# Bonus sums of a head pair as four float32 products on 32-column strips instead of two products with ones

## The chip, the cores and the metric

The kernel runs on one core of a Trainium2 chip. The metric is the device time of one execution in microseconds; three runs of the kernel before give a median of 993.13 us (991.97 to 993.62). Engines are called PE (matrix products), PEld (its weight loads), DVE (vector), ACT (scalar, activations), POOL (general) and SP (which issues most of the DMA transfers). Each engine has its own list of instructions and runs it in order; engines wait for one another by semaphores.

## What is computed

One layer of a hybrid encoder for 512 tokens behind 16 meta tokens, width 2048. One input projection gives the columns of two branches: a recurrence of 16 heads of 64 (RWKV-7) and a gated convolution. The part that matters here:

```python
kk = kk / maximum(norm(kk, axis=-1), 1e-12)        # per head and token: the key norm
k  = k * (1.0 + (a - 1.0) * k_a)
y  = recurrence(r, decay, k, v, kk, kk * a)
bonus = sum(r * k * r_k, axis=-1) * v              # per head and token: a sum over the head's 64 channels
y_a = (groupnorm(y) + bonus) * silu(g_r)
y_b = B * conv3(C * h) * silu(g_c)
h_res = h_res + concat(y_a, y_b) @ w_out
```

Both the key norm and the bonus are sums over the 64 channels of a head. Channels lie on partitions (two heads, a head pair, fill the 128), so such a sum goes over partitions and is done by PE as a product with a matrix of zeros and ones.

## The kernel before

**Projections.** 65 tiles of 128 output columns are streamed through PE, each as products over 16 slices of 128 inputs. A weight quarter (128 x 512) is split into a rounded high half and the rest as low half, and every product is made of three: high by high, high by low, low by high (`steps`, `pieces`). Raw weights come by SP into three buffers `wr` of two quarters (L159); ACT casts a quarter's high half (L151), DVE subtracts for the low half (L152), into six buffers `hl`. Names like w50 count these quarters; quarter 4j+q belongs to tile j of the plan. The plan runs k, r, v of two head pairs, their g, and then a convolution group C, h, B, gc; the first such group has B ahead of the plan.

**PE's order is written by hand.** `fill(ns)` takes projection products from the stream until their planned time is used up; between the calls stand the products of the head pairs. The time table `FW` sets how much projection work lies between them. The order of DVE, ACT, POOL and SP is made by a scheduler from priorities: `ahead()` raises a block of instructions, and weight splits are raised too.

**Head pairs.** `prepare(i)` does pair i, `invert` two of them. In `prepare`, after the low-rank paths, DVE forms the operands `ar` and `bk` and the product `r = r * hv * ta` (L734, the elementwise bonus). PE then makes the gram products (L754) and, in `gram_meta`, the key norms: four float32 products of 144 columns (L786), each with 32 columns of the constants as weights and each on its own strip of 32 columns of PE (`tile_position`), into one bank at columns 96 to 239. ACT copies them to `n2` (L779). SP sends `n2` to DRAM (`sn`), and reads it back spread over 72 partitions as `nd`; so the gram blocks go through `sg` and come back as `d`.

**The bonus before.** `split` casts r to its rounded half (ACT, L664) and subtracts (DVE, L665). After the gram products, two products of 512 columns with the 128 x 128 matrix `ones` (L818, L819; 1 within a head, 0 elsewhere) write the sums into the bank `zb`, already spread over the channels; ACT copies the bank to r (L820). DVE multiplies r by v (L917), and SP stores it for later (L918).

**Inversion.** From `nd` and `d`, DVE inverts 16 x 16 blocks, 72 at a time: two rows on nd (L853, L854), a copy to y (L859), tt and y (L860, L861), then for m = 2, 4, 8 blocks of four dependent rows: product, sum, product, sum (L871 to L886). The last row of a pair is the sum of 512 numbers per partition. y goes to DRAM (`sx`, L901) and comes back as `xT` and `xo` (L892, L893); DVE turns xT into `xn` (L946), and PE uses xn in the products t (L961), first for the even pair, then for the odd one. These steps have planned times on a clock that counts PE's products: the store of y at 29000 ns for an even pair and 20500 (22500 for pair 1) for an odd one.

**Convolution.** DVE takes C from its two banks to u (a row ex for four edge columns, and two rows u), later h to hh in the same way (L402, L403); POOL multiplies u by hh (L484); ACT makes cv (L486) and DVE adds two taps (L489). At the end of a group of two pairs the chain of the odd pair and this convolution share DVE with the splits.

Of the kernel before, what the change touches and what calls it, by code (L numbers as in the profile page):

```python
# [9 lines left out]
F32 = mybir.dt.float32  # L10
F32R = mybir.dt.float32r
I32 = mybir.dt.int32
AF = mybir.ActivationFunctionType
ALU = mybir.AluOpType
# [4 lines left out]
P = 128  # L19
DM = 2048  # L20
KT = DM // P
SEQ = 512
META = 16
L = SEQ + META
CH = 64
# [7 lines left out]
C_ID, C_GM, C_BM, C_ON = 0, 128, 384, 512  # L33
# [11 lines left out]
    tr=3200, lev=3000, cp=4200, out=1500, begin=19500, p=2900, u=2900, s=4200, mid=1000, last=3700, mix=2600,  # L45
# [44 lines left out]
def hymba_kernel(ctx: ExitStack, tc: tile.TileContext, xt, xtok, front, w_in, w_out, pv, lup, cst, msk, gf, out):  # L90
    nc = tc.nc
    ctx.enter_context(tc.manual_schedule(engines={mybir.EngineType.PE}))
    cp = ctx.enter_context(tc.tile_pool(name="cp", bufs=1))
    dp = ctx.enter_context(tc.tile_pool(name="dp", bufs=2, space=DRAM))
# [3 lines left out]
    cs = cp.tile([P, C_N], F32, name="cs")  # L98
# [13 lines left out]
    def col(off, i=0):  # L112
        return pvt[:, off + i : off + i + 1]
# [55 lines left out]
    xp = ph1.enter_context(tc.tile_pool(name="xp", bufs=1))  # L169
# [3 lines left out]
    rst = xp.tile([P, 4], F32, name="rst")  # L173
    rsx = cq.tile([P, 2 * META], F32, name="rsx")
    la = cq.tile([P, 2, L], F32R, name="la")
    ones = xp.tile([P, P], F32R, name="ones")
    omm = xp.tile([P, 33], F32, name="omm")
    hv = xp.tile([P, 6, 8], F32, name="hv")
    hl = cp.tile([P, 2, 8], F32, name="hl")
# [3 lines left out]
    pi = ph1.enter_context(tc.tile_pool(name="pi", bufs=1, space=PSUM))  # L183
# [5 lines left out]
    def tr(name, dt=F32):  # L189
        return cq.tile([P, LP], dt, tag="tr", name=name, bufs=5)  # L190
# [121 lines left out]
    with tc.issue_after(head):  # L312
        nc.vector.tensor_scalar(
            out=omm, in0=pvt[:, V_MU : V_MU + 33], scalar1=-1.0, scalar2=1.0, op0=ALU.mult, op1=ALU.add
        )
        for d, off in (
# [4 lines left out]
                out=d, in0=pvt[:, off : off + 8], scalar1=0.5, scalar2=None, op0=ALU.mult  # L321
            )
        nc.vector.tensor_scalar(
            out=hv[:, 4], in0=pvt[:, V_KA : V_KA + 8], scalar1=-0.5, scalar2=1.0, op0=ALU.mult, op1=ALU.add
        )

    nc.scalar.copy(ones, cs[:, C_BM : C_BM + P])
    FULL = ((0, 272), (272, L))
    TAIL = ((14, 272), (272, L))
    REAL = ((META, L),)  # L330
# [44 lines left out]
    def next_banks():  # L375
        what, i = plan[state["tile"] + 1]
        return [pm.tile([P, 512], F32, tag="main", name=f"ps_{what}{i}_{r}") for r in range(2)]
# [236 lines left out]
    def fill(ns):  # L614
        while ns > 0:
            seen = len(ready)
            t = step()
            if t is None:
                return
            ns -= t  # L620
            if len(ready) > seen:
                ns += FW["evac"]
# [23 lines left out]
    def ahead():  # L646
        return tc.high_priority(offset=AHEAD)

    def c3(t):
        return t.rearrange("p (c s) -> p c s", s=CH)  # L650
# [7 lines left out]
        nc.vector.tensor_tensor(out=lo, in0=raw, in1=hi.bitcast(F32), op=ALU.subtract)  # L658
        return hi, lo

    def split(t, name, n):
        hi = tr(f"{name}_h", F32R)[:, 0:n]
        lo = tr(f"{name}_l", F32R)[:, 0:n]
        nc.scalar.copy(hi, t)  # L664
        nc.vector.tensor_tensor(out=lo, in0=t, in1=hi.bitcast(F32), op=ALU.subtract)  # L665
        return hi, lo

    heads = [(h, slice(64 * h, 64 * h + 64), slice(64 - 64 * h, 128 - 64 * h)) for h in range(2)]

    place = [(i % 2) * 4 + i // 2 for i in range(NPAIR)]  # L670
# [11 lines left out]
    def behind(dst, src):  # L682
        with tc.issue_after(state["dma"]):
            nc.sync.dma_start(dst, src)
# [5 lines left out]
    def second_level(z):  # L690
        return [t[:, 256:512].rearrange("p (q k s) -> p q k s", q=2, s=32) for t in z]

    def prepare(i):
# [22 lines left out]
            out=bk[:, :, 0], in0=c3(k), scalar=hv[:, 2, i : i + 1], in1=c3(te), op0=ALU.mult, op1=ALU.mult  # L716
# [3 lines left out]
            out=ta, in0=ta, scalar1=hv[:, 3, i : i + 1], scalar2=hv[:, 4, i : i + 1], op0=ALU.mult, op1=ALU.add  # L720
        )
        nc.vector.scalar_tensor_tensor(
            out=ar[:, :, 0], in0=c3(k), scalar=col(V_KK, i), in1=e1[:, :, 0:CH], op0=ALU.mult, op1=ALU.mult
# [6 lines left out]
        r = got["r", i]  # L730
        nc.vector.tensor_tensor(
            out=ar[:, 1:NCH, 1], in0=c3(r), in1=e1[:, 1:NCH, 1 : CH + 1], op=ALU.mult
        )
        nc.vector.scalar_tensor_tensor(  # L734
            out=r, in0=r, scalar=hv[:, 5, i : i + 1], in1=ta[:, CH:LP], op0=ALU.mult, op1=ALU.mult
        )

        sq = tr(f"sq{i}")
        nc.scalar.activation(sq, k, AF.Square, scale=col(V_KK, i))
        rh, rl = split(r, f"rk{i}", SEQ)  # L740
        fill(FW["gram_b" if p else "gram"] + FW["meta"].get(i, 0))

        late = state["step"] > 48
# [16 lines left out]

        def gram_meta():
            z = early or next_banks()
            norms = key_norms(z[0][:, 96 : 96 + NS])
            for h, hs, ho in heads:
                nc.tensor.matmul(
                    z[h][:, 0:META],
                    bk[hs, 0, h : h + 2, :].rearrange("p a s -> p (a s)"),
                    ar[hs, 0, 0, 0:META],
                    start=True, stop=True,
                )  # L770
            if p and "levels" in state:
                state["out"] = state.pop("levels").pop(0)(second_level(z))
            with ahead():
                for h in range(2):
                    nc.vector.tensor_tensor(
                        out=gt[:, h, 0, 0:META], in0=z[h][:, 0:META], in1=gmask[:, h, 0:META], op=ALU.mult
                    )
            with ahead():
                nc.scalar.copy(n2, norms)  # L779
            if "out" in state:  # L780
                state.pop("out")()
            state["banks"] = z

        def key_norms(z):
            for j in range(4):
                nc.tensor.matmul(  # L786
                    z[32 * j : 32 * j + 32], cs[:, C_BM + 48 : C_BM + 80], sq[:, j * NS : (j + 1) * NS],
                    start=True, stop=True, tile_position=(0, 32 * j),
                )
            return z  # L790
# [11 lines left out]

        NS = LP // 4
        n2 = tr(f"n2{i}")[:, 0:NS]
        if late:
            gram_meta()
        za = [pz.tile([P, 4, P], F32, tag="tz", name=f"g{i}_1_{h}") for h in range(2)]
# [3 lines left out]
        if not late:  # L811
            gram_meta()
# [1 line left out]
        masked(zc, 5, 9)  # L814
        fill(FW["gram2"] - FW["meta"].get(i, 0))

        zb = pi.tile([P, SEQ], F32, tag="ser", name=f"zb{i}")
        nc.tensor.matmul(zb, ones[:, 0:P], rh, start=True, stop=False)  # L818
        nc.tensor.matmul(zb, ones[:, 0:P], rl, start=False, stop=True)  # L819
        nc.scalar.copy(r, zb)  # L820
        fill(FW["misc"])


# [4 lines left out]
        sg = dp.tile([SCR], F32, tag="sg", name=f"sg{i}")  # L828
        sn = dp.tile([2 * LP], F32, tag="sn", name=f"sn{i}")
        sx = scr_x[i % 2]  # L830

        def rows(t, h):
            return bass.AP(tensor=t.tensor, offset=t.offset + h * NCH * 4 * BLK, ap=[[CH, CH], [4 * BLK, NCH], [1, CH]])

        def blocks(t):
            return bass.AP(tensor=t.tensor, offset=t.offset, ap=[[BLK, 8 * NCH], [CH, 16], [1, 16]])

        for h in range(2):
            behind(sn[h * LP : (h + 1) * LP].rearrange("(j s) -> j s", s=NS), n2[16 - 16 * h : P : 32])
        for h in range(2):  # L840
            behind(rows(sg, h), gt[64 * h : 64 * h + 64, h, :, 0:CH])
        NB = 8 * NCH
# [5 lines left out]
        nd = cq.tile([NB, 16], F32, tag="nd", name=f"nd{i}")  # L848
        behind(d, blocks(sg))
        behind(nd, sn.rearrange("(p s) -> p s", s=16))  # L850
        y = cq.tile([NB, 256], F32, tag="y", name=f"y{i}").rearrange("p (s t) -> p s t", t=16)
        nc.gpsimd.memset(y, 0.0)
        nc.vector.tensor_scalar(out=nd, in0=nd, scalar1=1e-24, scalar2=None, op0=ALU.max)  # L853
# [9 lines left out]
        def sub(x, r0, c0, dims):  # L863
            return bass.AP(tensor=x.tensor, offset=x.offset + r0 * 16 + c0, ap=[list(x.ap[0])] + dims)

        for m in (2, 4, 8):
            for b in range(16 // (2 * m)):
# [4 lines left out]
                    out=pq,  # L872
                    in0=sub(d, o, o + m, [[16, m], [0, m], [1, m]]),
                    in1=sub(y, o + m, o + m, [[0, m], [1, m], [16, m]]),
                    op=ALU.mult,
                )
                nc.vector.tensor_reduce(
                    out=tq.rearrange("p (i j) -> p i j", i=m), in_=pq, op=ALU.add, axis=AX.X
                )
                nc.vector.tensor_tensor(  # L880
                    out=pq,
                    in0=sub(y, o, o, [[16, m], [0, m], [1, m]]),
                    in1=bass.AP(tensor=tq.tensor, offset=tq.offset, ap=[list(tq.ap[0]), [0, m], [1, m], [m, m]]),
                    op=ALU.mult,
# [19 lines left out]
        for h, hs, ho in heads:  # L904
            for b in range(2):
                for a in range(2):
                    later(9000 + 900 * (4 * h + 2 * b + a), lambda h=h, b=b, a=a: nc.sync.dma_start(
                        bass.AP(
                            tensor=bd.tensor,
                            offset=bd.offset + (h ^ a) * (NCH - 1) * CH * NPAIR * P + place[i] * P + 64 * h + 32 * b,  # L910
                            ap=[[NPAIR * P, 32], [32 * NPAIR * P, 2 * NCH - 2], [1, 32]],
# [11 lines left out]
        for b in range(4):  # L923
            for t in range(2):
                later(14000 + 1000 * (2 * b + t), lambda b=b, t=t: nc.sync.dma_start(
                    bass.AP(
                        tensor=vd.tensor,
                        offset=vd.offset + (64 * (1 - b // 2) + 32 * t) * NPAIR * CH + place[i] * CH + 32 * (b % 2),
                        ap=[[NPAIR * CH, 32], [P * NPAIR * CH, NCH], [1, 32]],
# [264 lines left out]
    for i in range(0, NPAIR, 2):  # L1194
        invert([prepare(i), prepare(i + 1)])
# [161 lines left out]
    def here(t, n):  # L1357
        return xa[t][:, n * 512 : (n + 1) * 512] if n < 2 else xb[n - 2][:, t]
# [153 lines left out]
    z = {}  # L1512
# [55 lines left out]
    with tc.manual_schedule(engines={mybir.EngineType.DVE, mybir.EngineType.Activation, mybir.EngineType.Pool}):  # L1568
# [16 lines left out]
        for part in range(2):  # L1585
            cols = slice(256 * part, 256 * part + 256)
            for jj in range(8):
                hi, lo = right[(1, "M2", jj // 2), jj % 2]
# [4 lines left out]
            h = here(1, 2)[:, cols]  # L1593
# [70 lines left out]
```

## Time and profile before

| | before |
|---|---|
| median of three runs | 993.13 us (991.97 to 993.62) |
| span of the profiled execution | 991.2 us |
| PE busy | 981.2 us (99%) |
| DVE busy | 707.8 us (71%) |
| ACT busy | 390.4 us (39%) |
| two products with ones, each | 0.39 us, x8 |
| ACT: cast for the split / copy of the sums | 0.62 / 0.587 us, x8 each |
| DVE: subtraction for the split / product with v | 0.69 / 0.69 us, x8 each |

The span is that of one execution under the profiler; times of runs are a little longer, since they hold what lies around the span. A row in order of time gives the start, the duration, the engine, the line, what is written from what, the shape, and in brackets how long the engine had been idle ahead of it and for whom it had waited. Durations of matmuls overlap: what a matmul costs PE is the distance from its start to the start of the next one. Buffer numbers are left out in the profile (w for w50, y for y1).

### The profile page before, as it was taken

What the parts mean: (1) busy time and instruction counts of PE and PEld (TensorE: products, weight loads), DVE (VectorE), ACT (ScalarE), POOL (GpSimd) and SP (SyncE); (2) the same over time, 40 slices, a digit from 0 to 9 for tenths busy, and PEclk for the clock granted to TensorE, in tenths of its full rate; (3) what the DMA queues carried; (4) which work ended last, traced back from release to release, by engine and by line L of the source; (5) the groups of instructions that cost most, each with busy time, mean ns of one, the idle gap of its engine ahead of it and who ended that gap; (6) DMA issues with size and microseconds to landing.
All of it is one profiled execution on the core that took longest, in us unless ns stands there. A gap on an engine that the chain in (4) does not pass through costs nothing.

```text
span 991.2 us, 23393 instructions
## 1 busy us (share of the span) xinstructions
PE 981.2 (99%) x9511; PEld 907.4 (92%) x9511; DVE 707.8 (71%) x1413; ACT 390.4 (39%) x731; POOL 128.0 (13%) x242
## 2 busy tenths in 40 slices
PE   9999999999999999999999999999999999999996
PEld 8999999999998999998999998889889898788885
DVE  6777966578675679653779654465756697998897
ACT  7553432344322434322434323232332435546464
POOL 0110302012010121010111010011211102001001
PEclk9999999999999999999999999999999999999999
DMA  9526576246675385853375856988886697697654
GB/s 324 156 91 149 145 202 160 88 126 150 152 181 166 92 194 117 211 150 107 87 186 122 205 143 189 280 250 250 229 252 189 179 281 197 183 313 197 149 128 170
DMA packets 205387, 176.89 MB, mean 178 GB/s; under 512 B 138528, under 2 KB 168032, under 8 KB 204768
## 3 DMA queue, kind: packets, MB, share of 16 engines
q1 hardware_dynamic: 202688, 166.50, 60.2%
q0 software_dynamic: 2304, 8.39, 4.9%
q8 instruction: 74, 1.21, 0.5%
q10 hardware_dynamic: 288, 0.52, 0.1%
q14 instruction: 33, 0.27, 0.1%
HBM read 139.02 MB, written 36.35 MB: 177 GB/s over the span
## 4 chain that ended last, share of the span: by engine, by line
PE 94%; DVE 3%; DMA 1%; ACT 1%; issue 1%; SPq 0%; DVEq 0%; POOL 0%; ACTq 0%
PE ps_v L352 9%; PE ps_h L352 9%; PE ps_C L352 9%; PE ps_g L352 9%; PE ps_gc L367 9%; PE ps_B L367 9%; PE ps_k L352 8%; PE ps_r L352 8%; PE M L1381 5%; PE P L1381 4%; PE Q L1381 2%; PE g L754 2%; PE ps_lora L367 1%; PE ps_k L367 1%; PE zy L1139 1%; PE ps_r L367 1%
## 5 line engine op out<-in xcount | busy, mean ns | idle before, releaser
L151 ACT CAST w<-wr 128x512 fp32r<-128x512 f32 x252 | 153.7, 619 | 285.8 <-PE ps_C L352 47.5
L152 DVE TENSOR_TENSOR w<-wr,w 128x512 fp32r<-128x512 f32 x252 | 175.3, 707 | 117.7 <-ACT w L151 116.7
L352 PE MATMUL ps_v<-xh,w 128*128 128x256 f32 (+2 forms) x512 | 84.0, 285 | 0.0
L367 PE MATMUL ps_B<-xh,w 128*128 128x512 f32 x256 | 83.4, 394 | 0.0
L352 PE MATMUL ps_h<-xh,w 128*128 128x256 f32 (+2 forms) x512 | 81.6, 281 | 0.0
L352 PE MATMUL ps_g<-xh,w 128*128 128x256 f32 (+2 forms) x512 | 81.5, 281 | 0.0
L367 PE MATMUL ps_gc<-xh,w 128*128 128x512 f32 x256 | 81.1, 392 | 0.0
L352 PE MATMUL ps_C<-xh,w 128*128 128x256 f32 (+2 forms) x512 | 80.8, 280 | 0.0
L352 PEld LDWEIGHTS ps_v<-xh,w 128*128 128x128 f32 x512 | 73.9, 188 | 0.3
L352 PE MATMUL ps_k<-xh,w 128*128 128x256 f32 (+1 forms) x448 | 73.4, 285 | 0.0
L352 PE MATMUL ps_r<-xh,w 128*128 128x256 f32 (+1 forms) x448 | 72.6, 281 | 0.0
L352 PEld LDWEIGHTS ps_h<-xh,w 128*128 128x128 f32 x512 | 72.1, 189 | 0.3
L352 PEld LDWEIGHTS ps_g<-xh,w 128*128 128x128 f32 x512 | 72.0, 189 | 0.4
L352 PEld LDWEIGHTS ps_C<-xh,w 128*128 128x128 f32 x512 | 71.7, 189 | 0.2
L352 PEld LDWEIGHTS ps_k<-xh,w 128*128 128x128 f32 x448 | 64.7, 188 | 0.4
L352 PEld LDWEIGHTS ps_r<-xh,w 128*128 128x128 f32 x448 | 63.5, 189 | 0.2
L352 PE MATMUL ps_h<-xl,w 128*128 128x256 f32 x256 | 57.3, 281 | 0.0
L367 PEld LDWEIGHTS ps_gc<-xh,w 128*128 128x128 f32 x256 | 47.8, 188 | 10.0
L367 PEld LDWEIGHTS ps_B<-xh,w 128*128 128x128 f32 x256 | 47.8, 188 | 9.7
L352 PE MATMUL ps_C<-xl,w 128*128 128x256 f32 x256 | 56.2, 280 | 0.0
L352 PE MATMUL ps_v<-xl,w 128*128 128x256 f32 x256 | 55.8, 278 | 0.0
L352 PE MATMUL ps_g<-xl,w 128*128 128x256 f32 x256 | 55.5, 278 | 0.0
(382 smaller groups left out, 2143.6 us busy)
## 6 DMA issues: line engine op xcount, KB each, us to landing
wr<-in_w_in_dram SPq DMA_DIRECT2D x126, 512.0 KB
ct<-opd SPq DMA_DIRECT2D x72, 192.0 KB
wo<-in_w_out_dram SPq DMA_DIRECT2D x24, 512.0 KB
x<-in_w_out_dram POOLq DMA_DIRECT2D x16, 512.0 KB, 5.7
opd<-ar SPq DMA_DIRECT2D x8, 576.0 KB
opd<-gt SPq DMA_DIRECT2D x16, 288.0 KB
bd<-bt SPq DMA_DIRECT2D x64, 64.0 KB
bw<-bd SPq DMA_DIRECT2D x16, 256.0 KB
```

Source lines behind the costliest of these rows:

```text
L151: nc.scalar.copy(hi, rq)
L152: low[q] = eng.tensor_tensor(out=lo, in0=rq, in1=hi.bitcast(F32), op=ALU.subtract).ins
L352: nc.tensor.matmul(ps[r][:, 0 : b - a], ww[:, k * P : (k + 1) * P], xx[:, kt, a:b], start=(kt == 0 and n == 0), stop=(kt == KT - 1 and n = ...
L367: nc.tensor.matmul(ps[r], ww[:, w], xx[:, kt, a:b], start=(kt == 0 and n == 0), stop=(kt == KT - 1 and n == 2))
L754: nc.tensor.matmul(z[h][:, c - c0], bk[hs, c, h : h + 2, :].rearrange("p a s -> p (a s)"), ar[hs, c].rearrange("p a s -> p (a s)"), start= ...
L1139: nc.tensor.matmul(zy[e][hs if e else ho, k], t[hs, o : o + CH], x, start=(n == 0), stop=(n == 2))
L1381: nc.tensor.matmul(bank[s], left(prod, jj, m, s), w, start=(jj == 0 and n == 0), stop=(jj == 7 and n == 2))
```

## The change

The matrix `ones`, `split`, the bank `zb`, the two products and the copy back from the bank are taken out. The sums of the bonus are now made like the key norms, right behind them: four float32 products of 128 columns on four strips, straight from r, into the pair's second bank. The function for both is `head_sums`. ACT copies the 128 columns to `nb`; SP stores four rows of it per head in `sb` and reads `sb` back into r, each head's row of 512 numbers spread over its 64 partitions (source pattern 2 x 64 times the same x 512). The product r times v waits for that transfer.

```diff
-    ones = xp.tile([P, P], F32R, name="ones")
...
-    nc.scalar.copy(ones, cs[:, C_BM : C_BM + P])
...
-    def split(t, name, n):
-        hi = tr(f"{name}_h", F32R)[:, 0:n]
-        lo = tr(f"{name}_l", F32R)[:, 0:n]
-        nc.scalar.copy(hi, t)
-        nc.vector.tensor_tensor(out=lo, in0=t, in1=hi.bitcast(F32), op=ALU.subtract)
-        return hi, lo
...
-        rh, rl = split(r, f"rk{i}", SEQ)
...
-            norms = key_norms(z[0][:, 96 : 96 + NS])
+            norms = head_sums(z[0][:, 96 : 96 + NS], sq, NS)
+            bonus = head_sums(z[1][:, 96 : 96 + P], r, P)
...
                 nc.scalar.copy(n2, norms)
+                nc.scalar.copy(nb, bonus)
...
-        def key_norms(z):
+        def head_sums(z, x, n):
             for j in range(4):
                 nc.tensor.matmul(
-                    z[32 * j : 32 * j + 32], cs[:, C_BM + 48 : C_BM + 80], sq[:, j * NS : (j + 1) * NS],
+                    z[32 * j : 32 * j + 32], cs[:, C_BM + 48 : C_BM + 80], x[:, j * n : (j + 1) * n],
                     start=True, stop=True, tile_position=(0, 32 * j),
                 )
...
-        zb = pi.tile([P, SEQ], F32, tag="ser", name=f"zb{i}")
-        nc.tensor.matmul(zb, ones[:, 0:P], rh, start=True, stop=False)
-        nc.tensor.matmul(zb, ones[:, 0:P], rl, start=False, stop=True)
-        nc.scalar.copy(r, zb)
...
+        sb = dp.tile([2 * SEQ], F32, tag="sb", name=f"sb{i}")
...
+        for h in range(2):
+            behind(sb[h * SEQ : (h + 1) * SEQ].rearrange("(j s) -> j s", s=P), nb[16 * h : P : 32])
...
         behind(nd, sn.rearrange("(p s) -> p s", s=16))
+        behind(r, bass.AP(tensor=sb.tensor, offset=sb.offset, ap=[[SEQ, 2], [0, CH], [1, SEQ]]))
```

PE's list changes only by these products; `FW` is as before. The scheduler's lists are others. In the rows below, the names carry buffer numbers, and the engine that a row waits for stands in brackets. The lines after the change are 6 or 7 lower than before.

DVE in the first convolution group, where the inversion of pair 1 meets h0 and gc0. Before, the last rows of y1 lie around hh0, the evacuation of h0:

```order
L871 TENSOR_TENSOR prod1_1872<-d1_1864,y1_1868 72x512 [waits DVE_49]
L877 TENSOR_REDUCE tt1_1873<-prod1_1872 72x64 [waits DVE_49]
L880 TENSOR_TENSOR prod1_1872<-y1_1868,tt1_1873 72x512 [waits DVE_49]
L403 TENSOR_TENSOR hh0_2136<-ps_h0_0_2016,rs_116 128x256 [waits PE_49]
L886 TENSOR_REDUCE y1_1868<-prod1_1872 72x8x8 [waits DVE_49]
L402 TENSOR_TENSOR ex_2137<-ps_h0_1_2017,rst_117 128x4 [waits PE_49,Pool_49]
L403 TENSOR_TENSOR hh0_2136<-ps_h0_1_2017,rs_116 128x256
L152 TENSOR_TENSOR w50_2010<-wr25_2008,w50_2010 128x512 [waits DMAHW2_49,Activation_49]
```

After, hh0 stands much earlier in y1's chain (behind three of its four smallest blocks), and the splits of w50 and w51 stand behind the chain's last row:

```order
L879 TENSOR_REDUCE y1_1870<-prod1_1874 72x2x2 [waits DVE_49]
L401 TENSOR_TENSOR hh0_2138<-ps_h0_0_2018,rs_116 128x256 [waits PE_49]
L864 TENSOR_TENSOR prod1_1874<-d1_1865,y1_1870 72x8 [waits DVE_49]
L870 TENSOR_REDUCE tt1_1875<-prod1_1874 72x4 [waits DVE_49]
L873 TENSOR_TENSOR prod1_1874<-y1_1870,tt1_1875 72x8 [waits DVE_49]
L879 TENSOR_REDUCE y1_1870<-prod1_1874 72x2x2 [waits DVE_49]
L864 TENSOR_TENSOR prod1_1874<-d1_1865,y1_1870 72x64 [waits DVE_49]
L870 TENSOR_REDUCE tt1_1875<-prod1_1874 72x16 [waits DVE_49]
L400 TENSOR_TENSOR ex_2139<-ps_h0_1_2019,rst_117 128x4 [waits PE_49,Pool_49]
L401 TENSOR_TENSOR hh0_2138<-ps_h0_1_2019,rs_116 128x256
```

So the wait for h0's first bank moved ahead of 15 rows of the chain, and what is behind the chain moved with it. On ACT the row cv0<-u0 moved from behind the casts of w50 and w51 to ahead of them.

DVE in the second group, where the inversion of pair 3 meets C1 and h1. Before, the row ex, which waits for the end of tile C1, stands in the middle of the chain:

```order
L859 COPY y3_3668<-nd3_3665 72x16 [waits DMAHW3_49,DVE_49,Pool_49]
L152 TENSOR_TENSOR w90_3748<-wr45_3746,w90_3748 128x512 [waits DMAHW2_49,Activation_49]
L152 TENSOR_TENSOR w91_3751<-wr45_3746,w91_3751 128x512 [waits Activation_49]
L860 TENSOR_TENSOR tt3_3673<-d3_3664,nd3_3665 72x8 [waits DMAHW3_49]
L861 TENSOR_TENSOR y3_3668<-tt3_3673,nd3_3665 72x8 [waits DVE_49]
L871 TENSOR_TENSOR prod3_3672<-d3_3664,y3_3668 72x8 [waits DVE_49]
L946 STREAM_TRANSPOSE xn2_4064<-xT2_3079 128x512 [waits DMAHW6_49]
L877 TENSOR_REDUCE tt3_3673<-prod3_3672 72x4 [waits DVE_49]
L880 TENSOR_TENSOR prod3_3672<-y3_3668,tt3_3673 72x8 [waits DVE_49]
L152 TENSOR_TENSOR w92_3780<-wr46_3778,w92_3780 128x512 [waits DMAHW4_49,Activation_49]
L886 TENSOR_REDUCE y3_3668<-prod3_3672 72x2x2 [waits DVE_49]
L402 TENSOR_TENSOR ex_3870<-ps_C1_1_3512,rst_117 128x4 [waits PE_49]
```

After, the product r times v (waiting for its transfer) and that ex stand ahead of w90, w91 and tt:

```order
L852 COPY y3_3674<-nd3_3670 72x16 [waits DVE_49,Pool_49]
L910 TENSOR_TENSOR r3_3151<-r3_3151,v3_3324 128x512 [waits DMAHW5_49]
L400 TENSOR_TENSOR ex_3876<-ps_C1_1_3513,rst_117 128x4 [waits PE_49]
L152 TENSOR_TENSOR w90_3754<-wr45_3752,w90_3754 128x512 [waits DMAHW6_49,Activation_49]
L152 TENSOR_TENSOR w91_3757<-wr45_3752,w91_3757 128x512 [waits Activation_49]
L853 TENSOR_TENSOR tt3_3679<-d3_3669,nd3_3670 72x8 [waits DMAHW7_49]
L854 TENSOR_TENSOR y3_3674<-tt3_3679,nd3_3670 72x8 [waits DVE_49]
```

The ex moved up by ten rows, past two splits and the start of the chain. Before, r3 times v stood far ahead, between the splits of w87 and w88. Later in the same chain, hh1 moved from behind its last row to ahead of it. In pair 5 (and 7 alike) both rows of pr_g and their ex, which stood behind tt, now stand ahead of it; in pair 0 r times v moved behind the copy y<-nd, where it stood in the other even pairs already.

SP for pair 3 (a count at the end of a row means several alike). Before:

```order
L684 DMA sn3_3659<-n23_3490 4x144 x2
L684 DMA sg3_3658<-gt3_3488 64x9x64 x2
L684 DMA nd3_3665<-sn3_3659 72x16
L159 DMA wr45_3746<-in_w_in_dram 128x1024
L684 DMA d3_3664<-sg3_3658 72x16x16
L159 DMA wr46_3778<-in_w_in_dram 128x1024
```

After:

```order
L675 DMA sn3_3661<-n23_3490 4x144 x2
L675 DMA sb3_3662<-nb3_3491 4x128 x2
L675 DMA sg3_3660<-gt3_3488 64x9x64 x2
L675 DMA nd3_3670<-sn3_3661 72x16
L675 DMA r3_3151<-sb3_3662 128x1x512
L159 DMA wr45_3752<-in_w_in_dram 128x1024
L675 DMA d3_3669<-sg3_3660 72x16x16
```

The three new transfers stand between the norms' store and the weights wr45; the one that spreads r is the last ahead of them.

More of the change, by code (lines that the diff above doesn't have):

```diff
@@ L804, in prepare @@
         n2 = tr(f"n2{i}")[:, 0:NS]
+        nb = tr(f"nb{i}")[:, 0:P]
         if late:
```

## The prediction

> **What bounds the kernel now.** I read the page first, then the rows of single engines in order of time around the places that the change moves.
>
> ```profile
> span 991.2 us, 23393 instructions
> PE 981.2 (99%) x9511; PEld 907.4 (92%) x9511; DVE 707.8 (71%) x1413; ACT 390.4 (39%) x731; POOL 128.0 (13%) x242
> L152 DVE TENSOR_TENSOR w<-wr,w 128x512 fp32r<-128x512 f32 x252 | 175.3, 707 | 117.7 <-ACT w L151 116.7
> L352 PE MATMUL ps_v<-xh,w 128*128 128x256 f32 (+2 forms) x512 | 84.0, 285 | 0.0
> ```
>
> PE is busy for 99% of the span, and the projections wait for nothing (0.0 idle). Two things can change the time: what PE has to do, and whether an operand comes late. DVE idles for 283 us in all, so the work taken from it is worth nothing by itself; what counts is whether the low half of a weight quarter (L152) or an inverse is ready when PE's fixed order reaches it.
>
> The profiled execution has a span of 991.2 us; the median run is 993.13, 1.9 us more. I work out a difference and put it on the median. About 2 us (0.2%) either way can't be told from no change.
>
> **PE's own work.** Per head pair the change removes the two products with ones and adds a second group like the one for the norms, right behind it.
>
> ```profile
> 84.16 0.45 PE L786 MATMUL ps_v<-sq,cs 128*32 128x144 f32 x8
> 84.55 0.40 PE L765 MATMUL ps_v<-ar,bk 64*128 64x16 f32 x4
> 88.74 0.40 PE L818 MATMUL zb<-rk_h,ones 128*128 128x512 f32 x1
> 88.98 0.40 PE L819 MATMUL zb<-rk_l,ones 128*128 128x512 f32 x1
> 89.22 0.28 PE L352 MATMUL ps_r<-xl,w 128*128 128x256 f32 x1
> ```
>
> From start to start the two old products take 89.22 - 88.74 = 0.48 us. The norm group of 4 x 144 columns takes 84.55 - 84.16 = 0.39, and the switch of tile shape is in that. The trace has no strip group behind another one. At most the new group costs a whole norm group again, 0.39, so that 0.09 is saved. At the least its 512 columns cost what 512 columns cost above, 0.24, so that 0.24 is saved. I take the norm group scaled to 128 columns, 0.39 x 128/144 = 0.35, since it is the same instruction: 0.13 saved per pair, **1.0 us** over eight pairs (0.7 to 1.9). That is real time, since PE is the bound.
>
> **ACT and DVE.** Per pair these rows go: the cast (0.62) and L820 (0.587) on ACT, L665 (0.69) on DVE. ACT gains one copy of 128 columns, priced by the copy of 144 at 0.28.
>
> ```profile
> L664 ACT CAST rk_h<-r x8: 620/622/624, 77.0 to 531.9; 128x512 fp32r<-128x512 f32 x8
> L665 DVE TENSOR_TENSOR rk_l<-r,rk_h x8: 682/691/693, 78.8 to 532.5; 128x512 fp32r<-128x512 f32 x8
> L820 ACT COPY r<-zb x8: 579/587/589, 89.5 to 548.2; 128x512 f32<-128x512 f32 x8
> L779 ACT COPY n<-ps_g x2: 278/280/281, 394.9 to 542.1; 128x144 f32<-128x144 f32 x2
> ```
>
> Over eight pairs that is 7.4 us less on ACT and 5.5 on DVE, all under PE's stream: I cost it at nothing. The new products need r straight from L734, earlier than rk_l was ready, so they add no wait on PE.
>
> **The new transfer and what it does to DVE's order.** The product with v (L917, 0.69 us) now waits for r to come back through DRAM, and the DVE order of the change is another one. Three swaps matter; in all of them a row that waits for PE now stands ahead of the inversion chain of the odd pair. That chain (L860 to L886) is a string of dependent rows.
>
> *First group, tiles h0 and gc0.* Rows of DVE, then PE and ACT:
>
> ```profile
> 141.70 0.16 DVE L402 TENSOR_TENSOR ex<-ps_C,rst 128x4 f32<-128x4 f32 x1 [1.40 <-PE ps_C L352]
> 145.28 0.11 DVE L877 TENSOR_REDUCE tt<-prod 72x4 f32<-72x8 f32 x1
> 148.16 0.27 DVE L871 TENSOR_TENSOR prod<-d,y 72x64 f32<-72x64 f32 x1
> 153.58 0.67 DVE L886 TENSOR_REDUCE y<-prod 72x64 f32<-72x512 f32 x1
> 154.23 0.41 DVE L403 TENSOR_TENSOR hh<-ps_h,rs 128x256 f32<-128x256 f32 x1
> 154.56 1.28 DVE L152 TENSOR_TENSOR w<-wr,w 128x512 fp32r<-128x512 f32 x2
> 151.26 0.62 PE L352 MATMUL ps_h<-xl,w 128*128 128x256 f32 x4
> 152.67 0.39 PE L367 MATMUL ps_gc<-xh,w 128*128 128x512 f32 x1
> 157.30 0.72 ACT L486 ACTIVATE cv<-u,pvt 128x512 f32<-128x512 f32 x1 [9.34 <-POOL u L484]
> ```
>
> Now ex stands ahead of nd, r times v, and w48 and w49, so the chain starts later. Moreover hh0 is put after three of the four smallest blocks, and its first half needs the bank that PE leaves at 151.26 + 0.62 = 151.9. So at 151.9 DVE still has a block of four small rows ahead of it (0.8 us) that it had behind it at 148.16. What follows: hh 0.4, that block 0.8, the rest of the chain from 148.16 to 154.25 without the hh in it (6.1 - 0.3 = 5.8), the second half of hh with its ex 0.4. That ends at 159.3, not at 154.25. Behind it stand the splits of w50 and w51, 0.64 each: the low half of w50 is ready at 159.9. Who waits: gc0 starts at 152.67 and uses 24 products of 0.227 for two quarters, so w50 is wanted at 158.1 and its low half two products later, at 158.6. PE stalls **1.3 us**. ACT's order moves too: cv0 goes ahead of the casts of w50 and w51. In its old place it began 2.7 us after hh; now hh ends near 154.1, cv0 near 157.5, the cast of w50 at 158.1, just in time. Bounds: 0 (DVE passes hh earlier than I read it) and 2.5 (hh waits and cv0 both cost in full).
>
> *Second group, tiles h1 and B1.* Again DVE, then ACT, PE, SP:
>
> ```profile
> 273.01 1.29 DVE L152 TENSOR_TENSOR w<-wr,w 128x512 fp32r<-128x512 f32 x2 [2.67 <-ACT w L151]
> 274.23 0.15 DVE L860 TENSOR_TENSOR tt<-d,nd 72x8 f32<-72x8 f32 x1
> 278.46 0.16 DVE L402 TENSOR_TENSOR ex<-ps_C,rst 128x4 f32<-128x4 f32 x1 [1.34 <-PE ps_C L352]
> 288.26 0.68 DVE L886 TENSOR_REDUCE y<-prod 72x64 f32<-72x512 f32 x1
> 289.78 0.41 DVE L403 TENSOR_TENSOR hh<-ps_h,rs 128x256 f32<-128x256 f32 x1
> 293.89 2.49 DVE L152 TENSOR_TENSOR w<-wr,w 128x512 fp32r<-128x512 f32 x4
> 298.04 0.71 DVE L946 STREAM_TRANSPOSE xn<-xT 128x512 f32<-128x512 f32 x1 [1.66 <-DMA xT<-sx]
> 291.68 0.73 ACT L486 ACTIVATE cv<-u,pvt 128x512 f32<-128x512 f32 x1 [10.42 <-POOL u L484]
> 289.44 0.39 PE L367 MATMUL ps_B<-xh,w 128*128 128x512 f32 x1
> 299.75 1.13 PE L961 MATMUL t<-xn,gt 64*64 64x32 f32 x64
> 268.04 0.52 SPq L159 DMA_DIRECT2D wr<-in_w_in_dram  x1
> 289.01 0.30 SPq L901 DMA_DIRECT2D sx<-y  x1
> 293.26 0.60 SPq L892 DMA_DIRECT2D xT<-sx  x1
> ```
>
> Here the ex that waits for PE until 278.46 stood in the middle of the chain, with w90, w91 and four chain rows done by then. Now it is ahead of w90, w91 and tt: w90 and w91 end at 279.9, xn2 and three small rows bring it to 281.0, w92 and w93 take 1.3, and the chain's bare rows from its first sum on take 8.7 (as from 145.28 to 154.25 above, less the hh in it). Between them lie the rows of g3, u1 and h1 (2.7 us). The chain ends at 293.7, not at 288.94. The second half of hh1 stands ahead of its last row (0.68), so it ends near 293.0, not at 290.19: 2.8 late. cv1, then the cast of w94, move with it: cv1 from 291.68 to 294.5, cast done at 295.8. On DVE two cv rows (1.5 us from cv1's end at 295.1) stand ahead of the split, so w94's low half is ready at 297.3. PE wants w94 at 289.44 + 24 x 0.227 = 294.9 and its low half at 295.4: a stall of **1.9 us**. Then xn3: sx is written at 293.7 and not at 289.01; xT is issued 2.5 to 4.2 us later (4.2 in the row, where SP had other work between), xn3 starts 4.8 after that (298.04 - 293.26) and ends near 301.7 to 303.4. PE wants it half into t, at 300.3 + 1.9 = 302.2. I add **0.3** (0 to 1.2). The second group costs 2.2, with bounds 0 and 4: 0 if w94's operands don't pass through this chain, and the 4.7 by which the chain is late if PE met all of it.
>
> *Groups of pairs 5 and 7.*
>
> ```profile
> 410.35 0.16 DVE L860 TENSOR_TENSOR tt<-d,nd 72x8 f32<-72x8 f32 x1
> 414.76 0.41 DVE L403 TENSOR_TENSOR pr_g<-ps_g,rs 128x256 f32<-128x256 f32 x1
> 432.70 0.70 DVE L946 STREAM_TRANSPOSE xn<-xT 128x512 f32<-128x512 f32 x1
> 435.79 1.14 PE L961 MATMUL t<-xn,gt 64*64 64x32 f32 x64
> ```
>
> Both halves of pr_g now stand ahead of tt. tt goes from 410.35 to about 415.2, though the splits between are then done: I put the chain's end 3.7 us later. xn5 has 436.3 - 433.4 = 2.9 us in hand, and was held by its place in the order rather than by its transfer, so some of the 3.7 is absorbed. I take 0 for both pairs (0 to 1 each).
>
> Even pairs: only pair 0 has r times v later than before, by one place of 0.69 us, and its result is stored at 29000 ns of the planned clock, not at 20500: 0.
>
> SP issues three more transfers per pair ahead of wr: sb twice and r. Priced by L901's 0.30 and L159's 0.52, wr leaves 1.1 to 1.6 us later. A wr issued at 268.04 was cast ahead of 273.01; 1.6 later is still ahead of 278.46, where DVE now waits. Cost nothing, if the transfer itself is short.
>
> **Sum**: -1.0 + 1.3 + 2.2 = +2.5. By the profiled execution 991.2 + 2.5 = 993.7 of span; on the median 993.13 + 2.5 = **995.6 us**.
>
> **Rivals.**
>
> *The spread is slow.* r<-sb writes 256 KB to 128 partitions from two rows of 2 KB.
>
> ```profile
> q1 hardware_dynamic: 202688, 166.50, 60.2%
> ```
>
> By this row 166.50 MB took 0.602 x 16 x 991.2 = 9547 us of single engines, 17.4 KB per us. 256 KB are then 15 us of one engine, 0.9 if 16 share it, 7.5 if it is cut by its two source rows. For: the source has only two rows. Against: nothing in the trace, which has no such transfer. Then w48 and w90, whose wr is issued behind it, come up to 7.5 us late; 268.04 + 1.6 + 7.5 + 4 gives w90 at 281 where DVE is free at 278.5, so the second group loses some 2 us more, the first some 1: 995.6 + 3 = 998.6.
>
> The Trainium skill, page "DMA: Bandwidth & Descriptors", section "Why a DMA increments its semaphore by 16 and not by 1", states that a transfer uses the largest number of engines up to 16 that divides the outermost dimension of both its sides. By that rule this one runs on two, and the sum would be the 998.6 of this rival. No row here shows it.
>
> *No stall: only PE's saving is left.* The place is the same two lists of DVE. If the row ahead (ex, hh) finds its bank done when DVE gets there, or the splits still make 158.6 and 295.4, PE never waits and the 1.0 stays: 992.1 (991.2 with the best strip price). For it: the typical split is many us early, and DVE has 29% idle time. Against: of the two quarters w94 has next to nothing in hand (split from 293.89 on, wanted at 294.9), and what precedes it is now longer. It decides at a chain end of 291.8 or earlier.
>
> *One stall only*, group one or group two: 993.13 - 1.0 + 1.3 = 993.4, or + 2.2 = 994.3.
>
> **Chances.** Both stalls, as summed: 0.36 (994.4 to 996.8 by itself). Slow spread on top: 0.27, 998.6. One stall: 0.16. No stall: 0.17. Strips at their lower price and no stall, or something unseen on the good side: 0.04, below 991.1. The range 991.8 to 999.0 leaves out the last and the far end of the slow spread. Slower by over 0.2% means above 995.1: 0.31 of the 0.36 and all of the 0.27, 0.58. Faster 0.04. The rest, 0.38, is within.
>
> **What would show it.** PE idle rows near 158.6 (ps_gc waiting for w of DVE) and near 295 (ps_B) of 1 to 2 us confirm the swaps; chain ends (last L886 row of pairs 1 and 3) near 159 and 294 confirm the arithmetic. r<-sb landing within 2 us of its issue refutes the slow spread; the DVE wait ahead of r times v shows its time. A norm-plus-bonus group of 0.74 us confirms the strip price. I am wrong if PE shows no idle there, or if it shows idle ahead of rows that I priced at nothing: t of pairs 5 and 7, or any L352 row waiting for a late wr.

## The result and the profile after

| | before | after |
|---|---|---|
| median | 992.29 us (5 runs, 991.97 to 993.62) | 1013.81 us (5 runs, 1011.76 to 1018.42) |
| ratio | | 1.0221, interval 1.0209 to 1.0233 |
| span of the profiled execution | 991.2 us | 1010.0 us (its run took 1011.76) |

The change makes the kernel 2.2% slower. The direction was forecast; the size was not: 1013.81 lies far above the range of 991.8 to 999.0.

The page of the kernel after, its spans, the chain that ended last, and three groups (idle ahead of a group, and for whom, stands behind the bar). The lines of the kernel after are 2 to 9 lower than before: the projections' L352 and L367 are L350 and L365, the key norms' L786 is L778.

```profile
span 1010.0 us, 23492 instructions
PE 985.4 (98%) x9559; PEld 910.3 (90%) x9559; DVE 701.7 (69%) x1405; ACT 381.0 (38%) x722; POOL 125.4 (12%) x242
PE 69%; DVE 12%; DMA 11%; SPq 3%; ACT 2%; issue 2%; POOL 1%; DVEq 0%; ACTq 0%
L151 ACT CAST w<-wr 128x512 fp32r<-128x512 f32 x252 | 152.1, 619 | 300.4 <-DMA wr<-in_w_in_dram 72.5
L365 PE MATMUL ps_B<-xh,w 128*128 128x512 f32 x256 | 86.7, 407 | 3.4 <-ACT w L151 2.5
L365 PE MATMUL ps_gc<-xh,w 128*128 128x512 f32 x256 | 81.3, 392 | 2.7 <-DVE w L152 2.7
```

The casts of the weights now wait 72.5 us for their transfers; before, it was 19.5, and the releaser that ended most of their idle time was PE (47.5 us). The same lines before, with ACT's wait for these transfers:

```profile
PE 94%; DVE 3%; DMA 1%; ACT 1%; issue 1%; SPq 0%; DVEq 0%; POOL 0%; ACTq 0%
L151 ACT CAST w<-wr 128x512 fp32r<-128x512 f32 x252 | 153.7, 619 | 285.8 <-PE ps_C L352 47.5
ACT w L151 <- DMA wr<-in_w_in_dram: 19.5, 8, 3.8
```

The total of 72.5 shows that weights come late, but not what it costs: in the run with 4 source rows below it is 76.1 us, and that run is 14.6 us faster. The chain that ended last goes through DMA for 11% of the span, where it was 1%. PE's waits by releaser (total, times, longest):

```profile
PE t L954 <- DVE xn L939: 5.7, 2, 3.1
PE ps_gc L365 <- DVE w L152: 2.7, 1, 2.7
PE ta L632 <- ACT tz L637: 2.5, 2, 1.6
PE ps_B L365 <- ACT w L151: 2.5, 1, 2.5
PE ta L632 <- ACT tz L639: 1.0, 1, 1.0
PE ps_B L365 <- DVE w L152: 0.9, 1, 0.9
```

They sum to 15.3 us; before, PE waited for nothing between 80 and 560 us. All four convolution groups are hit, and three low-rank products ta. What came late is seen in pair 3. SP, DVE and ACT in order of time (start, duration, in brackets the idle time ahead):

```profile
273.81 0.56 SPq L675 DMA_DIRECT2D r<-sb  x1
274.42 0.47 SPq L159 DMA_DIRECT2D wr<-in_w_in_dram  x1
276.27 3.18 SPq L159 DMA_DIRECT2D wr<-in_w_in_dram  x1
281.53 0.69 DVE L910 TENSOR_TENSOR r<-r,v 128x512 f32<-128x512 f32 x1 [5.53 <-DMA r<-sb]
282.86 0.62 ACT L151 CAST w<-wr 128x512 fp32r<-128x512 f32 x1 [12.02 <-DMA wr<-in_w_in_dram]
```

r lands 7.2 us after its issue has ended (281.53 - 274.37). The weights issued right behind it are cast 8.0 us after theirs (282.86 - 274.89); before, w90's pair was issued at 268.56 and cast at 272.36, 3.8 us later:

```profile
268.04 0.52 SPq L159 DMA_DIRECT2D wr<-in_w_in_dram  x1
272.36 1.19 ACT L151 CAST w<-wr 128x512 fp32r<-128x512 f32 x2 [3.76 <-DMA wr<-in_w_in_dram]
```

After, the DMA engines are not full all the while (stretches of 2 us; the last two columns are their mean busy share and GB/s):

```profile
275.00:277.00 2.00, 2.00 (x20) 2.00 (x19) 0.60 (x3) 0.00 (x0) 0.00 (x0) 1.00 0.65 168
279.00:281.00 2.00, 2.00 (x20) 2.00 (x19) 0.00 (x0) 0.00 (x0) 0.00 (x0) 1.00 0.50 129
281.00:283.00 2.00, 2.00 (x20) 2.00 (x19) 0.76 (x2) 0.14 (x1) 0.33 (x2) 1.00 0.87 284
```

The share falls to 0.50 while weights are waited for, and rises to 0.87 when r is through. The bytes don't fill the engines. The packets of the trace show what happens. The 128 packets of 2 KB that carry r run two at a time, from 275.15 to 280.97. Of the 128 packets of 4 KB that carry the wr behind it, 112 start between 275.51 and 277.95. The other 16, which would be the share of two engines of 16, have not started at 280, when r is nearly through; the cast follows at 282.86. So most of the weights have come early, and the rest waits behind r. By the Trainium skill, page "DMA: Bandwidth & Descriptors", section "Why a DMA increments its semaphore by 16 and not by 1", a transfer is carried by the largest number of engines up to 16 that divides the outermost dimension of both sides, two here. The trace agrees with it: in each of the eight pairs r's packets are on average 1.9 to 2.1 at a time.

One more loss is in PE's clock. Behind three of the stalls the granted clock (third column from the right) is 0.50 for 3.41 us; before, it is 1.00 from 4 to 986 us:

```profile
157.00:160.00 3.00, 0.29 (x3) 0.05 (x1) 2.93 (x5) 1.08 (x2) 0.00 (x0) 1.00 0.56 95
160.00:163.00 3.00, 3.00 (x13) 2.49 (x14) 2.96 (x5) 0.00 (x0) 0.97 (x1) 1.00 0.72 186
302.48:305.89 3.41, 3.41 (x9) 2.67 (x8) 0.85 (x3) 0.00 (x0) 0.31 (x2) 0.50 0.70 143
449.26:452.67 3.41, 3.41 (x14) 3.02 (x13) 1.18 (x4) 1.61 (x4) 0.19 (x1) 0.50 1.02 404
602.86:606.27 3.41, 3.41 (x11) 2.76 (x10) 1.69 (x4) 1.14 (x2) 0.72 (x2) 0.50 0.88 336
```

What a clock of 0.50 takes away is half of the 3.41 us: 1.7 behind each of the three stalls, 5.1 in all. The stall at 157 (2.7 us by the waits) cost no clock.

### The profile page after: what moved, and what is told of

It reads as the page before. It is cut to its first block, busy times and chain, and to the rows that moved or that the text cites. A ratio compares the mean times of both kernels' runs of the same rounds, so it can differ in the third digit from the quotient of the medians.

```text
span 1010.0 us, 23492 instructions
## 1 busy us (share of the span) xinstructions
PE 985.4 (98%) x9559; PEld 910.3 (90%) x9559; DVE 701.7 (69%) x1405; ACT 381.0 (38%) x722; POOL 125.4 (12%) x242
## 4 chain that ended last, share of the span: by engine, by line
PE 69%; DVE 12%; DMA 11%; SPq 3%; ACT 2%; issue 2%; POOL 1%; DVEq 0%; ACTq 0%
PE ps_B L365 9%; PE ps_gc L365 8%; PE ps_v L350 7%; PE ps_k L350 6%; PE ps_C L350 5%; PE ps_g L350 5%; PE ps_r L350 5%; PE ps_h L350 5%; PE M L1374 5%; DMA wr<-in_w_in_dram 4%; DMA d<-sg 2%; PE P L1374 2%; DVE w L152 2%; DVE o L1343 1%; SPq L675 1%
## 5 line engine op out<-in xcount | busy, mean ns | idle before, releaser
L151 ACT CAST w<-wr 128x512 fp32r<-128x512 f32 x252 | 152.1, 619 | 300.4 <-DMA wr<-in_w_in_dram 72.5
L365 PE MATMUL ps_B<-xh,w 128*128 128x512 f32 x256 | 86.7, 407 | 3.4 <-ACT w L151 2.5
L350 PE MATMUL ps_v<-xh,w 128*128 128x256 f32 (+2 forms) x512 | 84.1, 285 | 0.0
L365 PE MATMUL ps_gc<-xh,w 128*128 128x512 f32 x256 | 81.3, 392 | 2.7 <-DVE w L152 2.7
L350 PE MATMUL ps_h<-xh,w 128*128 128x256 f32 (+2 forms) x512 | 82.5, 283 | 0.0
L350 PE MATMUL ps_g<-xh,w 128*128 128x256 f32 (+2 forms) x512 | 81.1, 281 | 0.0
L350 PE MATMUL ps_C<-xh,w 128*128 128x256 f32 (+2 forms) x512 | 80.8, 280 | 0.0
L350 PEld LDWEIGHTS ps_v<-xh,w 128*128 128x128 f32 x512 | 74.0, 188 | 0.3
L350 PE MATMUL ps_k<-xh,w 128*128 128x256 f32 (+1 forms) x448 | 73.0, 285 | 0.0
L350 PEld LDWEIGHTS ps_h<-xh,w 128*128 128x128 f32 x512 | 72.7, 190 | 0.3
L350 PE MATMUL ps_r<-xh,w 128*128 128x256 f32 (+1 forms) x448 | 72.4, 281 | 0.0
L350 PEld LDWEIGHTS ps_g<-xh,w 128*128 128x128 f32 x512 | 71.8, 189 | 0.1
L350 PEld LDWEIGHTS ps_C<-xh,w 128*128 128x128 f32 x512 | 71.8, 189 | 0.2
L350 PEld LDWEIGHTS ps_k<-xh,w 128*128 128x128 f32 x448 | 64.5, 188 | 0.3
L350 PEld LDWEIGHTS ps_r<-xh,w 128*128 128x128 f32 x448 | 63.4, 189 | 0.0
L365 PEld LDWEIGHTS ps_B<-xh,w 128*128 128x128 f32 x256 | 49.8, 196 | 14.6 <-ACT w L151 2.9
L365 PEld LDWEIGHTS ps_gc<-xh,w 128*128 128x128 f32 x256 | 47.7, 188 | 13.1 <-DVE w L152 3.1
L350 PE MATMUL ps_h<-xl,w 128*128 128x256 f32 x256 | 57.3, 281 | 0.0
L350 PE MATMUL ps_C<-xl,w 128*128 128x256 f32 x256 | 56.2, 280 | 0.0
L350 PE MATMUL ps_v<-xl,w 128*128 128x256 f32 x256 | 55.8, 278 | 0.0
L350 PE MATMUL ps_g<-xl,w 128*128 128x256 f32 x256 | 55.4, 278 | 0.0
```

The costliest lines, as they stand in the source:

```text
L151: nc.scalar.copy(hi, rq)
L350: nc.tensor.matmul(ps[r][:, 0 : b - a], ww[:, k * P : (k + 1) * P], xx[:, kt, a:b], start=(kt == 0 and n == 0), stop=(kt == KT - 1 and n = ...
L365: nc.tensor.matmul(ps[r], ww[:, w], xx[:, kt, a:b], start=(kt == 0 and n == 0), stop=(kt == KT - 1 and n == 2))
```

## The experiments

All ratios are to the kernel before, run on the same chip.

**Two transfers.** The source of each is one row, read by 64 partitions.

```diff
-        behind(r, bass.AP(tensor=sb.tensor, offset=sb.offset, ap=[[SEQ, 2], [0, CH], [1, SEQ]]))
+        for h in range(2):
+            behind(r[64 * h : 64 * h + 64], bass.AP(tensor=sb.tensor, offset=sb.offset + h * SEQ, ap=[[0, CH], [1, SEQ]]))
```

> The change, with the spread of r cut into two transfers, one for each head (64 partitions each, every partition reading the same 2 KB row); DVE's order moves a little with it. Slow spread (theory A: one transfer with two source rows is carried by few DMA engines, and everything that waits for it or is queued behind it is late): r lands within 2.5 us of its issue instead of 7.2 to 7.8, the waits of r times v (28.0 us in all after the change) fall below 5 us, and the time falls to 992 to 996. Order alone (theory B: the scheduler's other order of DVE costs the time, the transfer is incidental): the time stays above 1006 whatever r does.

992.26 us, ratio 0.9997 (0.9988 to 1.0006). The same bytes in two pieces, and the whole loss is gone. In pair 3 of that run:

```profile
268.73 1.13 SPq L675 DMA_DIRECT2D r<-sb  x2
272.29 0.69 DVE L911 TENSOR_TENSOR r<-r,v 128x512 f32<-128x512 f32 x1 [1.33 <-DMA r<-sb]
```

r lands 2.4 us after the second issue, and all waits for r sum to 1.8 us, as theory A had it. But this run has another order of DVE (some 80 of its 1405 rows stand elsewhere), so by itself it neither excludes theory B nor prices the order that the change really has; the runs with 16 and 4 rows do.

**Nobody waits.** The slow transfer goes to a buffer that nobody reads.

```diff
-        behind(r, bass.AP(tensor=sb.tensor, offset=sb.offset, ap=[[SEQ, 2], [0, CH], [1, SEQ]]))
+        dump = cq.tile([P, SEQ], F32, tag="dump", name=f"dump{i}")
+        behind(dump, bass.AP(tensor=sb.tensor, offset=sb.offset, ap=[[SEQ, 2], [0, CH], [1, SEQ]]))
```

> The change, with the slow transfer kept but landing in a buffer that nobody reads; r times v then takes the r that was not summed, so the bonus is left out of the result in its summed form. DVE's order is that of the change but for the place of r times v. If DVE's own wait for r makes the loss: 995 to 1000. If what is queued behind the transfer on the same engines (weights, d) makes it: 1005 to 1013. If the order of DVE makes it: above 1005 too, but the weights then land as early as before.

1011.95 us, ratio 1.0201 (1.0182 to 1.0220): practically the whole loss remains, and its interval overlaps that of the change. DVE's 28 us of waits for r, the most conspicuous new row of the profile, are worth about 2 us, if anything. What is left is what is queued behind the transfer, for which ACT still waits 71.4 us in total, or the order of DVE, which the runs with 16 and 4 rows hold fixed.

**The kernel before with a slow transfer.**

```diff
         behind(nd, sn.rearrange("(p s) -> p s", s=16))
+        dump = cq.tile([P, SEQ], F32, tag="dump", name=f"dump{i}")
+        behind(dump, bass.AP(tensor=sn.tensor, offset=sn.offset, ap=[[SEQ, 2], [0, CH], [1, SEQ]]))
```

> The kernel before, with one more transfer of the same form per pair (two rows of 2 KB from the norms' buffer spread over 128 partitions into a buffer that nobody reads), issued behind nd. Nothing is left out. If the transfers queued behind the slow one come late and that alone stalls PE: 998 or more, with rows of PE waiting for w. If only DVE's wait for r or its order costs: 992 to 995.

1006.8 us, ratio 1.0149 (1.0121 to 1.0177). Without the strips of the bonus, and with an order near that of before (some 80 of 1413 DVE rows stand elsewhere), the transfer costs 14 us. The profiled execution is the slowest of the four, 1011.4 us with a span of 1008.8. Its main waits of PE:

```profile
PE t L963 <- DVE xn L948: 5.0, 3, 2.3
PE ps_B L367 <- ACT w L151: 1.8, 1, 1.8
PE ps_B L367 <- DVE w L152: 0.9, 1, 0.9
```

With three of 0.2 to 0.3 they are 8.5 us, and the clock is 0.50 for 17.1 us, which takes another 8.5: together 17.0 of the 17.6 us by which this span is longer than that before.

**The same from 16 rows.** Its counterpart, with the order of every engine unchanged:

```diff
-        behind(dump, bass.AP(tensor=sn.tensor, offset=sn.offset, ap=[[SEQ, 2], [0, CH], [1, SEQ]]))
+        behind(dump, bass.AP(tensor=sn.tensor, offset=sn.offset, ap=[[32, 16], [0, 8], [1, SEQ]]))
```

> The kernel before with one more transfer per pair, as in the run before_spread and with the same order on every engine, but from 16 overlapping rows to 8 partitions each instead of 2 rows to 64. Nothing is left out. If the number of source rows is the cause: 992 to 995 where 2 rows gave 1006.8. If a further 256 KB per pair is enough by itself: 1003 or more.

992.33 us, ratio 0.9994 (0.9984 to 1.0003). 256 KB more per pair are free, if the outermost dimension of the source is 16 and not 2.

**No spread.** The line that spreads r is taken out.

> The change without the transfer that spreads r (r times v takes the r that was not summed: the summed bonus is left out). The strips and the stores of sb stay. PE's own saving of 1.0 us shows here if there is no stall: 991 to 993 by theory A. By theory B (order of DVE) stalls of PE at w50 and w94 of 1 to 2 us each remain: 994 to 997.

990.35 us, ratio 0.9976 (0.9967 to 0.9985), a little below the 991 to 993 expected, and a PE that waits for nothing of note. This shows PE's saving by itself. The group of products in pair 0:

```profile
83.08 0.45 PE L778 MATMUL ps_v<-sq,cs 128*32 128x144 f32 x8
83.34 0.40 PE L778 MATMUL ps_v<-r,cs 128*32 128x128 f32 x8
83.68 0.40 PE L756 MATMUL ps_v<-ar,bk 64*128 64x16 f32 x4
```

Norms and bonus together take 83.68 - 83.08 = 0.60 us, where the norms alone took 0.39. The bonus adds 0.21, for 0.48 that went away: 0.27 per pair, 2.2 us in all. That agrees with the 2.3 us between this run and the kernel before. The order of DVE did not stay that of the change here, so the run says nothing on the stalls that were forecast.

**16 rows and 4 rows.** The order of every engine is exactly that of the change, and so are the bytes; only the source pattern differs.

```diff
-        behind(r, bass.AP(tensor=sb.tensor, offset=sb.offset, ap=[[SEQ, 2], [0, CH], [1, SEQ]]))
+        behind(r, bass.AP(tensor=sb.tensor, offset=sb.offset, ap=[[32, 16], [0, 8], [1, SEQ]]))
```

> The change with the order of every engine's instructions unchanged and the same bytes moved; only the source pattern of the transfer into r is another: 16 overlapping rows, each to 8 partitions, in place of 2 rows, each to 64 (so r gets wrong numbers for most partitions). If the number of source rows sets how many DMA engines carry it, r lands within 2.5 us and the time is what the order of DVE alone makes: by the prediction's sum 993 to 997 (stalls near w50 and w94 of 1.3 and 2.2 us, less PE's saving). If the order alone made the loss, or the number of rows did not matter: 1008 or more.

> As the run with 16 rows, with 4 source rows, each to 32 partitions. If engines are as many as source rows, r takes about half of the 7.2 to 7.8 us that it took with 2 rows to land (4 to 5 us), and the time lies between: 996 to 1003. If the number of rows does not matter: 1008 or more.

16 rows: 993.11 us, ratio 1.0004 (0.9995 to 1.0013). 4 rows: 999.25 us, ratio 1.0063 (1.0049 to 1.0077). So 2, 4 and 16 rows give 1013.8, 999.3 and 993.1 us, with nothing else changed. In pair 3 of the run with 16 rows r is issued at 269.30 and the weights right behind it (SP, DVE and ACT in order of time):

```profile
269.30 0.55 SPq L675 DMA_DIRECT2D r<-sb  x1
269.90 0.59 SPq L159 DMA_DIRECT2D wr<-in_w_in_dram  x1
274.06 0.69 DVE L910 TENSOR_TENSOR r<-r,v 128x512 f32<-128x512 f32 x1 [2.57 <-DMA r<-sb]
275.47 1.14 ACT L151 CAST w<-wr 128x512 fp32r<-128x512 f32 x2 [6.45 <-DMA wr<-in_w_in_dram]
```

While these weights are moved, the same columns as above read:

```profile
273.00:275.00 2.00, 2.00 (x20) 2.00 (x19) 0.69 (x1) 0.00 (x0) 0.14 (x1) 1.00 1.07 288
```

The weights are cast 5.0 us after their issue, not 8.0, and the engines are full (1.07) where they were half idle. r took 4.2 us to land, not the 2.5 that were expected, and with 4 rows 5.6 to 6.7 in place of 4 to 5: the landing does not go down in proportion to the rows. The packets of pair 3 show why. With 2, 4 and 16 rows they are on average 1.9, 3.6 and 7.6 at a time, and take 5.8, 4.1 and 3.0 us from the first to the last; another 1.3 to 1.5 us lie outside them in each run (0.8 from the issue to the first packet, the rest behind the last). With 16 rows other packets run on the same engines, and one of r takes 0.11 us (median) in place of 0.08. PE's waits with 16 rows:

```profile
PE ps_gc L365 <- DVE w L152: 1.5, 1, 1.5
PE ps_B L365 <- DVE w L152: 0.9, 1, 0.9
```

These are the two stalls of the forecast, alone and at their places.

**The slow transfer two places later** on SP, behind wr and d of its pair and ahead of the next wr.

```diff
-        behind(r, bass.AP(tensor=sb.tensor, offset=sb.offset, ap=[[SEQ, 2], [0, CH], [1, SEQ]]))
+        later(3500, lambda: nc.sync.dma_start(r, bass.AP(tensor=sb.tensor, offset=sb.offset, ap=[[SEQ, 2], [0, CH], [1, SEQ]])))
...
-        nc.vector.tensor_tensor(out=r, in0=r, in1=v[:, CH:LP], op=ALU.mult)
-        later(12500, lambda: nc.sync.dma_start(rbd[i], r))
+        def add_bonus():
+            nc.vector.tensor_tensor(out=r, in0=r, in1=v[:, CH:LP], op=ALU.mult)
+            nc.sync.dma_start(rbd[i], r)
+
+        later(12500, add_bonus)
```

> The change with the slow transfer (2 source rows) issued two places later on SP, behind the weights and d of its pair and ahead of the next weights; r times v is asked for later as well. Nothing is left out. If the loss comes from what is queued behind the transfer: the weights that were behind it land 4 to 5 us earlier, the loss falls by a third or more, 997 to 1006. If the time of the transfer itself or the load on the memory makes it: unchanged, 1010 to 1016.

1006.61 us, ratio 1.0140 (1.0125 to 1.0155). This is just above the 997 to 1006 expected. A third of the loss goes (7.2 of the 20.7 us above the run with 16 rows): PE's waits sum to 11.1 us, not 15.3, and the clock falls once, not three times. That the rest stays because the next weights are behind the transfer now is likely, but not shown; the order of DVE moved too, in some 40 rows.

**Two transfers and two pins**, which beats both kernels. hh0 and hh1 are put behind the last big product of the inversion, and cv0 behind the cast of w51.

```diff
+        high[q] = nc.scalar.copy(hi, rq).ins
...
+            with behind_of("cast"):
                 nc.scalar.activation(cv, u[:, 0:SEQ], AF.Copy, scale=col(V_CW, i))
...
+                state["cast"] = high[4 * j + 7]
...
+        if i in (1, 3):
+            state["turned"] = last.ins
```

> The spread in two transfers, and two pins in the first and second convolution group: hh0 and hh1 behind the product of 512 numbers of the inversion, and cv0 behind the casts of w50 and w51 on ACT. Nothing is left out. If the stalls that remain with two transfers (1.5 us at w50, 0.6 at w94) come from the places of hh0 and cv0, the first goes to below 0.5 and the time to 990.5 to 991.8; if they come from the late start of the chain, it stays at 992 to 993.

990.63 us, ratio 0.9982 (0.9973 to 0.9991), 0.2% faster than before, with the bonus in full. With two transfers alone PE had waited 1.5 us at gc0 and 0.6 at B1; now the first is gone:

```profile
PE ps_B L365 <- DVE w L152: 0.7, 1, 0.7
```

Which of the pins does it was not tried apart.

## Why the prediction was wrong

**The step that failed** is the price of the transfer that spreads r. The sum put the new transfers at nothing "if the transfer itself is short", a condition that no row bore out, and where the rival of the slow spread dropped it, its price was far too small: "the second group loses some 2 us more, the first some 1: 995.6 + 3 = 998.6", with a chance of 0.27. That rival's mechanism was the one that happened: two engines, and weights late behind them. That its time of landing came out too (7.5 worked out, 7.2 in pair 3) is in part luck: the 7.5 are the packets alone, and these took 5.8; the rest lies before and behind them. Its chance was too low and its price too small by a factor of seven: between 16 rows and 2 rows, with one order, lie 1013.81 - 993.11 = 20.7 us. I had followed w48 and w90 only, and had asked what two transfers behind it lose, not what a queue loses that is held up once in each of eight pairs. In the profiled executions, 1010.0 - 991.4 = 18.6 us apart, it goes like this: PE's waits rise from 2.4 to 15.3 (12.9), the clock behind three stalls takes 5.1, and 0.6 is left over. Of the waits, 5.7 are t for xn of pairs 5 and 7, which I had priced at nothing with 2.9 us in hand; 3.5 are ta waiting for tz; the rest are the stalls at w50 and w94, 1.2 and 2.5 us longer than with 16 rows.

That the clock would fall was no step of the prediction at all. The spread of the runs goes with it, though not strictly: 1011.76 us at a mean clock of 0.993, 1018.42 at 0.986, but 1013.59 at 0.989 and 1015.94 at 0.990.

**The sum for a fast spread.** The run with 16 rows is exactly its case: 995.6 forecast, 993.11 measured.

- *PE's saving*: 1.0 forecast with bounds of 0.7 to 1.9, 2.2 measured. The assumption that failed is that a second group behind the first would pay the whole norm group again, scaled to its columns (0.35). It adds 0.21, less than the lower bound of 0.24. That the switch to strips and back, which was in the 0.39, is paid once would fit; no run shows it apart.
- *w50*: 1.3 forecast, 1.5 measured, in part by luck: the chain ended at 158.73 (159.3 worked out), but PE began gc0 at 151.86 and not at 152.67, so that the two errors nearly cancel.
- *w94*: 1.9 forecast, 0.9 measured. (The bound above for this group is given as 4, but its own reason makes 4.7.) The chain ended 0.55 us earlier than worked out (293.15, not 293.7), and cv1 with it. And PE began B1 at 289.86, not at 289.44: the stall at w50, less the saving, had put off the time at which w94 was wanted. I carried the late operand through, but not the late consumer.
- *xn3*: 0.3 forecast, 0.

So the order of DVE did what the prediction said, at the two places that it named, and costs about what PE saves: +2.4 - 2.2, beside a measured +0.3.

**ACT and DVE at nothing**: right as to DVE's wait (nobody waits: 1011.95 to 1013.81). The three SP issues were costed at nothing "if the transfer itself is short"; the condition was the whole matter, as said above.

## What to carry to other kernels

Before a transfer is put ahead of urgent ones in a queue, look at the outermost dimension of both its sides: here 2, 4 and 16 source rows made 1013.8, 999.3 and 993.1 us with the same bytes and the same order. Price a slow transfer by all that is queued behind it, in every turn of the loop, and not by who reads it: the reader's 28 us of waits were worth about 2, if anything. And where PE is the bound, a stall of 3 us may cost nearly 5, since the clock may fall behind it.

## What was not expected of the hardware

- SP itself is held up: the issue of the second wr behind the slow transfer took 3.18 us, where the same one took 1.44 before. The longest wr issue in pairs 5 and 7 took 4.93, and 2.04 in the whole run before. With 4 rows it is 5.62, though, in a much faster run, so this time does not price the loss either.
- The clock fell behind three of the stalls (single waits of 2.5, 2.6 and 3.1 us by the trace, the first with another of 0.9 within 2 us of it), and not behind one of 2.7. In the kernel before with the slow transfer it fell with no single wait above 2.3. The Trainium skill, page "TensorE: Matmul & The Clock Gate", section "What's actually happening", has the clock halve after an idle window of about 3.4 us. The trace agrees in the half; but here shorter waits were followed by it, and one of like length was not. The three falls last 3.41 us each and start 146.8 and 153.6 us apart, 43 and 45 times 3.41 within 0.2, so they lie on one grid. What decides whether a stall costs clock was not tried.
